# Row-wise inverse, Pool's large operations given to VectorE and ScalarE, the decay in the state update, and ScalarE in source order, in a one-layer RWKV-7 and Conformer step

## The chip, the cores and the metric

The kernel runs on one core of a Trainium2 chip. The metric is the device time of one execution in microseconds. The kernel before was timed three times: 1833.41, 1838.17 and 1839.06 us, median 1838.17. The engines are called by the profile's names: PE (TensorE, matrix products), PEld (its weight loads), DVE (VectorE), ACT (ScalarE), POOL (GpSimd) and SP (SyncE, which issues nearly all DMAs here).

## The reference, cut to what matters

520 columns are worked on together: 512 prompt tokens and 8 single decode tokens. After an RMSNorm, one product with `w_in` gives everything that the two branches need.

```python
proj = xn @ w_in                    # 2048 -> 3200 + 1024 + 2048 + 1024 + 4096
xs = p_shift + mu * (prev - p_shift)        # token shift, then r, k, v and two low ranks
decay = exp(-exp(w_log));  a = sigmoid(a0 + xa @ a_lora_b)
kk = k*k_k / max(norm(k*k_k), 1e-12);  kf = k * (1 + (a-1)*k_a)
# scan over tokens, 16 heads of 64 x 64 state:
S = S*w_t + (S a_t) b_t' + v_t k_t'         # a_t = -kk, b_t = kk*a
o_t = S r_t
o = groupnorm(o)*lnx_g + lnx_b + sum(r*kf*r_k)*v
y_a = (o * silu(gate_a)) @ w_proj_a
u = glu;  c = depthwise_conv31(u) + conv_b  # Conformer branch
y_b = (silu(layernorm(c)) * silu(gate_b)) @ w_proj_b
h = x + (sigmoid(ga)*y_a + sigmoid(gb)*y_b) @ w_out
h = h + sigmoid(h @ w_ple_gate) * (p @ w_ple);  y = rmsnorm(h)
```

All is float32. The scan also has an initial state for the 8 decode tokens; shifted rows, states and the last rows of the convolution's input are outputs as well.

## The kernel before, in words

**The large products.** Channels lie on the 128 partitions, the 520 columns along the free axis. Each tile of 128 output channels takes one `gemm` (L215), whose steps (`step`, L195) each multiply one 128 x 128 block of the weights with two halves of 260 columns. Both sides are split into a high and a low part (fp32r), so a step is three products of two halves, six matmuls. Weights come by DMA in tiles `w` (L141). For each group of four steps ACT writes the high part `wh` (L154), and DVE the low part `wl` (L169) by a subtraction. `wh` and `wl` have four buffers each; the high part is written three groups ahead of use (AHEAD, L31) and the low part is issued at the start of a later group (`lower`, L199).

**What lies beside them.** Everything else is written as Python generators that `tick` (L181) moves on by one piece after each step of a product. `yield 4` means "go on four steps later". `yield ROOM` means "go on when DVE has room": the program keeps a planned clock for PE and one for DVE, charges DVE `0.14 + 0.00107 n` us for an operation on n elements of a partition (L103), charges DVE `0.0007 n` us for an operation of POOL on more than 64 (L104), and holds a ROOM piece back while DVE's clock is over 1 us (LAG) ahead of PE's. This decides at build time in which order instructions are written. PE (L73) and, from L349 on, DVE keep that order on the chip (`manual_schedule`); the order of ACT, POOL and SP is chosen by the compiler's scheduler from its own cost model. On every engine instructions start in their queue's order, so one that waits holds back those behind it.

**One pass of `wkv` (L429), eight in all, two heads each.** It normalises `kk`, forms `ep` and `em` (running decays and their inverses, L480 to L484), `b`, `kf` (L488), `rk` and `bv` (the bonus, L503 to L506), and the scaled operands `ar` and `bk` (L511 to L518): per chunk of 64 tokens and head, rows of r, kk, kf and b times decays. Products of these, masked, give `nba`, `nbr` and the lower half of `ar` (L527 to L541). A 64 x 64 unit triangular matrix per chunk and head is inverted by its 32 x 32 diagonal blocks: the blocks go through DRAM (`nd`) into `ni`, one block on each partition; 31 steps of one multiplication `tm` and one sum `ti` (L566 to L571) build the inverse; it returns through DRAM (`td`) into `tts`, is transposed on DVE to `d11`, and matmuls form the off-diagonal block (`aux<-d,nba`, L587; `aux<-tts,yt`, L603). `ttb` holds the whole inverse. The loop over 8 chunks (L633 to L657) carries the state: four matmuls with `suv`, ACT copies `xs` (L640), one matmul per chunk with `ttb`, ACT copies into `suv` (L644), four matmuls with `bkt` and `nbr`, then DVE writes the next state twice, into `suv` and into `sf` (L653, L656). Between these three parts lie `ly` = 4 steps. The outputs are normalised per head, transposed, scaled by ACT to `og` (L689), and POOL adds `bv` and multiplies with the gate `sl` (L690, L691).

**What runs beside a pass.** `conv` (L713) makes 30 DVE operations on `c`, each a shifted multiply and add over 482 to 511 columns, all ROOM pieces. `scaled` (L370) empties a product's PSUM into `p`. `silu` (L393) and L918 have their products on POOL. While the last pass runs, `sample` (L751) does the decode tokens' state update with large operations of POOL and DVE. The helper lines L66 and L67 record every DVE, POOL and small-matmul instruction, so the profile shows them all under L67; they are told apart by the tiles' names.

Of the kernel before, what the change touches and what calls it, by code (L numbers as in the profile page):

```python
# [17 lines left out]
P = 128  # L18
# [52 lines left out]
def body(nc, tc, a):  # L71
    with ExitStack() as es:
# [34 lines left out]
        def tt(eng, out, x, y, op):  # L107
            eng.tensor_tensor(out, x, y, op=op)
# [240 lines left out]
        order.enter_context(tc.manual_schedule(engines={mybir.EngineType.DVE}))  # L349
# [60 lines left out]
        tts = kq.tile([P, NCH, 64], F32, name="tts")  # L410
        ttb = kq.tile([P, NCH, P], F32, name="ttb")
        nbrs = [kq.tile([P, NCH, P], F32, name=f"nbr{i}") for i in range(2)]
        for x in (tts, ttb, *nbrs):
            gps.memset(x, 0.0)
        d11 = kq.tile([P, NCH, 32], F32, name="d11")

        flag = {"samples": 0, "inv": -1, "done": -1, "loop": -1, "conv": 0, "yp": None, "merged": False}
# [11 lines left out]
        def wkv(p, box):  # L429
# [58 lines left out]
            gps.tensor_scalar(kf, av, col(O_KA, p), oka[:, p:p + 1], op0=ALU.mult, op1=ALU.add)  # L488
            tt(gps, kf, kf, k, ALU.mult)
            yield 5  # L490
# [3 lines left out]
            yield ROOM  # L494
            rk = gt("rk")
# [60 lines left out]
            gps.tensor_copy(epl, ep[:, :, 64])  # L556
            tt(gps, bh, bh, ep[:, :, 64:65].to_broadcast([P, NCH, P]), ALU.mult)
# [6 lines left out]
            gps.tensor_scalar(ti.rearrange("p i t -> p (i t)"), ttinit, 1.0, 0.0, op0=ALU.mult, op1=ALU.add)  # L564
            yield 3
            for t in range(1, 32):  # L566
                tm = kq.tile([P, 8, 32], F32, name="tm")
                tt(vec, tm[:, :, :t + 1], ti[:, :, :t + 1],
                   ni[:, 0:t + 1, t].unsqueeze(1).to_broadcast([P, 8, t + 1]), ALU.mult)
                vec.tensor_reduce(ti[:, :, t], tm[:, :, :t + 1], axis=AX.X, op=ALU.add)  # L570
                yield ROOM  # L571
            flag["inv"] = p
            for g in range(4):
                dma(out=td.rearrange("h c e i t -> (h c e) i t")[:, g * 8:(g + 1) * 8, :], in_=ti[g * 32:(g + 1) * 32])
            for h in range(2):
                for e in range(2):
                    dma(out=tts[h * 64 + e * 32:h * 64 + e * 32 + 32, :, e * 32:e * 32 + 32],
                        in_=td[h, :, e].rearrange("c i t -> i c t"))
            yield 16
            for h in range(2):  # L580
                vec.transpose(d11[h * 64:h * 64 + 32], tts[h * 64:h * 64 + 32, :, 0:32])
            yield 4
            o = aux().rearrange("p (c x) -> p c x", x=64)
            for c in range(NCH):
                for h in range(2):
                    x, y = quarter(2 * h), quarter(2 * h + 1)
                    pe.matmul(o[y, c, 0:32], lhsT=nba[x, c, 32:64], rhs=d11[x, c, :], start=True, stop=True)  # L587
# [12 lines left out]
            for c in range(NCH):  # L600
                for h in range(2):
                    x, y = quarter(2 * h), quarter(2 * h + 1)
                    pe.matmul(o[x, c, 0:32], lhsT=yt[y, c, :], rhs=tts[y, c, 32:64], start=True, stop=True)  # L603
            for h in range(2):
                s = half(h)
                gps.tensor_scalar(ttb[s, :, s], tts[s], 1.0, 0.0, op0=ALU.mult, op1=ALU.add)
# [24 lines left out]
            sf = kq.tile([P, 64], F32, name="sf", bufs=2)  # L631
            gps.memset(sf, 0.0)
            for c in range(NCH):  # L633
# [16 lines left out]
                if c + 1 < NCH:  # L650
                    for h in range(2):
                        s = half(h)
                        vec.scalar_tensor_tensor(suv[s, h, c + 1, :], sf[s], epl[s, c:c + 1], x[s, 3, :], op0=ALU.mult, op1=ALU.add)  # L653
                s0 = sf
                sf = kq.tile([P, 64], F32, name="sf", bufs=2)
                vec.scalar_tensor_tensor(sf, s0, epl[:, c:c + 1], x[:, 3, :], op0=ALU.mult, op1=ALU.add)  # L656
# [30 lines left out]
            og = gt("og")[:, :NPR]  # L687
# [4 lines left out]
            dma(out=oa_d[p, :, 0:NPR], in_=og)  # L692

# [19 lines left out]
        def conv(i, u):  # L713
# [417 lines left out]
```

## Time and profile before

| what | value |
|---|---|
| time of the profiled execution | 1836.85 us |
| its span, first to last instruction | 1835.1 us |
| median of the three runs | 1838.17 us |
| PE busy | 1785.5 us, 97% |
| DVE busy | 1279.5 us, 70% |
| ACT busy | 743.3 us, 41% |
| POOL busy | 353.3 us, 19% |

"Busy" is the union of an engine's instructions. Matmuls overlap one another, so a busy PE says that its queue did not run dry, and the number of matmuls in a stretch says how fast it went. The clock column (PEclk) is the share of full speed that the chip granted PE. In a row of waits stand the waiting instruction, what released it, the sum in us, how often, and the longest.

### The profile page before, as it was taken

The numbers are of one execution on the slowest core, as the hardware profiler recorded it, in microseconds if no ns is written. First come the engines' busy times: TensorE is split into PE (matmuls) and PEld (weight loads), VectorE is DVE, ScalarE is ACT, GpSimd is POOL, SyncE is SP. The second block draws the span as 40 slices with busy tenths as digits, with TensorE's granted clock in tenths as the row PEclk, the third lists the DMA queues.
The fourth block names the chain that finished last, engine by engine and source line by source line (L and its number), as shares of the span: only waits on it lengthen the run. The fifth ranks groups of instructions, "written<-read, shape, count | busy, mean of one in ns | idle before, by whom it ended". The sixth has DMA issues, their size and how long they took to land.

```text
span 1835.1 us, 37880 instructions
## 1 busy us (share of the span) xinstructions
PE 1785.5 (97%) x15576; PEld 1744.7 (95%) x15576; DVE 1279.5 (70%) x2300; ACT 743.3 (41%) x1355; POOL 353.3 (19%) x370
## 2 busy tenths in 40 slices
PE   9999999999999999999999999999999999999996
PEld 9999999999998999989999999999999999999995
DVE  6569999799798797896996998465444333334456
ACT  6735336244253363353362332454333222243354
POOL 1222203113113013032131155001022000011102
PEclk9999999999999999999999999999999999999998
DMA  6252322532432433324323344467555433362232
GB/s 232 84 133 79 107 93 79 114 92 74 119 103 68 112 96 98 96 80 107 94 84 104 122 131 149 130 225 238 192 179 185 123 116 98 93 195 93 93 104 94
DMA packets 121037, 220.49 MB, mean 120 GB/s; under 512 B 47888, under 2 KB 56208, under 8 KB 120864
## 3 DMA queue, kind: packets, MB, share of 16 engines
q1 hardware_dynamic: 119264, 216.47, 38.4%
q8 instruction: 122, 2.00, 0.4%
q10 hardware_dynamic: 1600, 1.60, 0.3%
q14 instruction: 51, 0.42, 0.1%
HBM read 188.69 MB, written 29.34 MB: 119 GB/s over the span
## 4 chain that ended last, share of the span: by engine, by line
PE 74%; DVE 19%; issue 3%; ACT 1%; POOL 1%; DMA 1%; SPq 0%; DVEq 0%; ACTq 0%; POOLq 0%
PE mm L211 68%; PE aux L67 5%; DVE wl L67 4%; DVE tm L67 4%; DVE c L67 3%; DVE ti L67 2%; PE aux L211 1%; DVE p L67 1%; DVE sq L67 1%; DVE on L67 1%; PE oc L67 1%; DMA w<-in_win 0%; DVE h L67 0%; DVE suv L67 0%; DVE m L67 0%
## 5 line engine op out<-in xcount | busy, mean ns | idle before, releaser
L154 ACT ACTIVATE wh<-w 128x512 fp32r<-128x512 f32 (+1 forms) x541 | 338.7, 628 | 627.5 <-PE mm L211 503.8
L211 PE MATMUL mm<-xh,wh 128*128 128x260 f32 x2784 | 589.1, 293 | 0.4 <-ACT xh L266 0.4
L211 PE MATMUL mm<-xh,wl 128*128 128x260 f32 x2784 | 565.9, 285 | 4.6 <-DVE wl L67 4.6
L211 PE MATMUL mm<-xl,wh 128*128 128x260 f32 x2784 | 566.0, 285 | 0.3 <-DVE xl L67 0.3
L67 DVE TENSOR_TENSOR wl<-w,wh 128x512 fp32r<-128x512 f32 (+1 forms) x541 | 397.5, 738 | 200.4 <-ACT wh L154 198.3
L211 PEld LDWEIGHTS mm<-xh,wh 128*128 128x128 f32 x2784 | 432.6, 191 | 12.1 <-ACT wh L154 0.6
L211 PEld LDWEIGHTS mm<-xh,wl 128*128 128x128 f32 x2784 | 433.7, 191 | 5.2 <-DVE wl L67 5.2
L211 PEld LDWEIGHTS mm<-xl,wh 128*128 128x128 f32 x2784 | 433.8, 191 | 0.6 <-DVE xl L67 0.5
L211 PE MATMUL mm<-hi,wl 128*128 128x260 f32 x1600 | 333.5, 284 | 2.6 <-DVE wl L67 2.6
L211 PE MATMUL mm<-hi,wh 128*128 128x260 f32 x1600 | 333.3, 283 | 0.0
L211 PE MATMUL mm<-lo,wh 128*128 128x260 f32 x1600 | 332.4, 282 | 0.0
L211 PEld LDWEIGHTS mm<-hi,wl 128*128 128x128 f32 x1600 | 250.7, 189 | 3.1 <-DVE wl L67 3.1
L211 PEld LDWEIGHTS mm<-hi,wh 128*128 128x128 f32 x1600 | 252.0, 189 | 0.1
L211 PEld LDWEIGHTS mm<-lo,wh 128*128 128x128 f32 x1600 | 251.8, 189 | 0.0
L67 DVE SCALAR_TENSOR_TENSOR c<-u,prm,c 128x482 f32<-128x482 f32 (+14 forms) x240 | 201.6, 840 | 4.4
L67 DVE TENSOR_TENSOR tm<-ti,ni 128x16 f32<-128x16 f32 (+30 forms) x248 | 104.1, 420 | 4.9
L67 POOL TENSOR_TENSOR sq<-hi,lo 128x520 f32<-128x520 f32 (+1 forms) x20 | 24.3, 1220 | 337.8 <-DVE one L67 184.0
L67 DVE TENSOR_TENSOR p<-mm,rs 128x520 f32<-128x520 f32 x78 | 53.7, 689 | 48.3 <-PE mm L211 48.2
L67 DVE TENSOR_REDUCE ti<-tm 128x8 f32<-128x16 f32 (+30 forms) x248 | 73.6, 297 | 8.5
L67 DVE TENSOR_TENSOR s<-mm,s 128x520 f32<-128x520 f32 x32 | 22.4, 700 | 65.9 <-PE mm L211 65.9
L67 POOL COPY nsh<-p 128x9 f32<-128x9 f32 x25 | 14.9, 597 | 238.0 <-DVE p L67 238.0
L67 DVE SCALAR_TENSOR_TENSOR suv<-sf,epl,aux 64x64 f32<-64x64 f32 x112 | 31.1, 278 | 38.4 <-PE aux L67 22.4
(233 smaller groups left out, 1652.5 us busy)
## 6 DMA issues: line engine op xcount, KB each, us to landing
w<-in_win SPq DMA_DIRECT2D x170, 512.0 KB, 3.7
w<-in_wout SPq DMA_DIRECT2D x32, 512.0 KB, 3.7
w<-in_wpg SPq DMA_DIRECT2D x24, 512.0 KB, 3.7
s<-sga_d SPq DMA_DIRECT2D x32, 260.0 KB, 2.8
w<-in_wpa SPq DMA_DIRECT2D x16, 512.0 KB, 3.8
w<-in_wpb SPq DMA_DIRECT2D x16, 512.0 KB, 3.8
wx<-in_wpg SPq DMA_DIRECT2D x32, 256.0 KB, 3.5
x<-in_xT SPq DMA_DIRECT2D x16, 260.5 KB, 5.7
```

The source lines that it names most:

```text
L67: return f(*args, **kw)
L154: behind.append(act(wh[:, k], w[:, k], AF.Copy))
L211: nc.tensor.matmul(o[h], lhsT=w[:, used[0] % 4, :], rhs=x[:, h * HF:(h + 1) * HF], start=(k == 0 and i == 0), stop=(k == nk - 1 and i == 2))
```

## The change

It does six things.

- **ACT in source order.** `manual_schedule` at L349 takes ACT as well as DVE: until the product with `w_proj_a` is done (L967) ACT's queue is in the order in which the program is written.
- **The inverse by rows.** The steps run from row 30 to row 0 and take `ni[:, t, t:]`, a contiguous row, where they took `ni[:, 0:t+1, t]`, a column with 32 elements between neighbours. Steps and lengths are the same (31, of 2 to 32 times 8 elements). The inverse comes back into `dtt`, and one DVE transpose of 128 partitions makes `dt`; before, two of 32 partitions made `d11`, and `tts` served as the other form.
- **POOL's large operations elsewhere.** To DVE: the product `kf*k`, half of `ar` and half of `bk` (four operations a pass), the two operations on `og` (now one fused multiply and add that reads PSUM, and one product), the decode columns' product in `conv` and the running sum `csum`. To ACT: `kf`'s scale and bias, `epl`, the initial `ti`, the four diagonal blocks of `ttb`, and the bias of `og`, now put on `bv`.
- **The decay in the state update.** `bk` is no longer multiplied by the chunk's decay. The update is `(x + S) * epl`: DVE forms `suv` from `x`, `epl` and an `sf` that ACT has already scaled; `sf` is no longer computed by DVE in each chunk.
- **No tile of its own for `og`.** It is written over `bv`. A pass waits, before `rk`, until the output of the pass two before it has been issued.
- **Some pauses** are moved or added (16 steps become 18 after the inverse, and ROOM stands before each product of `ar` and `bk`).

```diff
-        order.enter_context(tc.manual_schedule(engines={mybir.EngineType.DVE}))
+        order.enter_context(tc.manual_schedule(engines={mybir.EngineType.DVE, mybir.EngineType.Activation}))
...
-            gps.tensor_scalar(kf, av, col(O_KA, p), oka[:, p:p + 1], op0=ALU.mult, op1=ALU.add)
-            tt(gps, kf, kf, k, ALU.mult)
-            yield 5
+            act(kf, av, AF.Identity, scale=col(O_KA, p), bias=oka[:, p:p + 1])
+            yield 3
+            tt(vec, kf, kf, k, ALU.mult)
+            yield 1
...
             yield ROOM
+            while p > 1 and flag["out"] < p - 2:
+                yield 1
             rk = gt("rk")
...
+            act(bv[:, :NPR], bv[:, :NPR], AF.Identity, bias=col(O_LB, p))
...
                 tt(vec, ar[h][s, :, h, :], ch(kk)[s], ep[s, :, 0:64], ALU.mult)
-                tt(gps, ar[h][s, :, 1 - h, :], ch(r)[s], ep[s, :, 1:65], ALU.mult)
+                yield ROOM
+                tt(vec, ar[h][s, :, 1 - h, :], ch(r)[s], ep[s, :, 1:65], ALU.mult)
                 yield ROOM
                 tt(vec, bk[s, :, h, :], ch(b)[s], ch(em)[s], ALU.mult)
-                tt(gps, bk[s, :, 1 - h, :], ch(kf)[s], ch(em)[s], ALU.mult)
+                yield ROOM
+                tt(vec, bk[s, :, 1 - h, :], ch(kf)[s], ch(em)[s], ALU.mult)
...
-            gps.tensor_copy(epl, ep[:, :, 64])
-            tt(gps, bh, bh, ep[:, :, 64:65].to_broadcast([P, NCH, P]), ALU.mult)
+            act(epl, ep[:, :, 64], AF.Copy)
...
-            gps.tensor_scalar(ti.rearrange("p i t -> p (i t)"), ttinit, 1.0, 0.0, op0=ALU.mult, op1=ALU.add)
+            act(ti.rearrange("p i t -> p (i t)"), ttinit, AF.Copy)
...
-            for t in range(1, 32):
+            for t in range(30, -1, -1):
                 tm = kq.tile([P, 8, 32], F32, name="tm")
-                tt(vec, tm[:, :, :t + 1], ti[:, :, :t + 1],
-                   ni[:, 0:t + 1, t].unsqueeze(1).to_broadcast([P, 8, t + 1]), ALU.mult)
-                vec.tensor_reduce(ti[:, :, t], tm[:, :, :t + 1], axis=AX.X, op=ALU.add)
+                tt(vec, tm[:, :, t:], ti[:, :, t:], ni[:, t:t + 1, t:].to_broadcast([P, 8, 32 - t]), ALU.mult)
+                vec.tensor_reduce(ti[:, :, t], tm[:, :, t:], axis=AX.X, op=ALU.add)
                 yield ROOM
...
-                    dma(out=tts[h * 64 + e * 32:h * 64 + e * 32 + 32, :, e * 32:e * 32 + 32],
-                        in_=td[h, :, e].rearrange("c i t -> i c t"))
-            yield 16
-            for h in range(2):
-                vec.transpose(d11[h * 64:h * 64 + 32], tts[h * 64:h * 64 + 32, :, 0:32])
+                    dma(out=dtt[h * 64 + e * 32:h * 64 + e * 32 + 32], in_=td[h, :, e].rearrange("c t i -> t c i"))
+            yield 18
+            dt = kq.tile([P, NCH, 32], F32, name="dt")
+            vec.transpose(dt, dtt)
...
-                gps.tensor_scalar(ttb[s, :, s], tts[s], 1.0, 0.0, op0=ALU.mult, op1=ALU.add)
+            for q in map(quarter, range(4)):
+                act(ttb[q, :, q], dt[q], AF.Copy)
...
-                        vec.scalar_tensor_tensor(suv[s, h, c + 1, :], sf[s], epl[s, c:c + 1], x[s, 3, :], op0=ALU.mult, op1=ALU.add)
-                s0 = sf
-                sf = kq.tile([P, 64], F32, name="sf", bufs=2)
-                vec.scalar_tensor_tensor(sf, s0, epl[:, c:c + 1], x[:, 3, :], op0=ALU.mult, op1=ALU.add)
+                for h in range(2) if c + 1 < NCH else ():
+                    s = half(h)
+                    if c:
+                        vec.scalar_tensor_tensor(suv[s, h, c + 1, :], x[s, 3, :], epl[s, c:c + 1], sf[s], op0=ALU.mult, op1=ALU.add)
+                    else:
+                        vec.tensor_scalar(suv[s, h, 1, :], x[s, 3, :], epl[s, 0:1], None, op0=ALU.mult)
+                for h in range(2) if c + 1 < NCH else ():
+                    act(sf[half(h)], suv[half(h), h, c + 1, :], AF.Copy, scale=epl[half(h), c + 1:c + 2])
+                if c + 1 == NCH:
+                    vec.scalar_tensor_tensor(sf, x[:, 3, :], epl[:, c:c + 1], sf, op0=ALU.mult, op1=ALU.add)
...
-            act(og, ot, AF.Identity, scale=col(O_LG, p), bias=col(O_LB, p))
-            tt(gps, og, og, bv[:, :NPR], ALU.add)
-            tt(gps, og, og, sl[:, :NPR], ALU.mult)
+            yield 1
+            vec.scalar_tensor_tensor(og, ot, col(O_LG, p), bv[:, :NPR], op0=ALU.mult, op1=ALU.add)
+            tt(vec, og, og, sl[:, :NPR], ALU.mult)
...
-            tt(gps, tm, sc, cw.unsqueeze(1).to_broadcast([P, NS, 31]), ALU.mult)
+            tt(vec, tm, sc, cw.unsqueeze(1).to_broadcast([P, NS, 31]), ALU.mult)
...
-                tt(gps, csum, csum, c, ALU.add)
+                tt(vec, csum, csum, c, ALU.add)
```

More of the change, by code (lines that the diff above doesn't have):

```diff
@@ L408, in lowrank @@
             flag["low"] = True
-        tts = kq.tile([P, NCH, 64], F32, name="tts")
         ttb = kq.tile([P, NCH, P], F32, name="ttb")
         nbrs = [kq.tile([P, NCH, P], F32, name=f"nbr{i}") for i in range(2)]
-        for x in (tts, ttb, *nbrs):
+        for x in (ttb, *nbrs):
             gps.memset(x, 0.0)
-        d11 = kq.tile([P, NCH, 32], F32, name="d11")
-        flag = {"samples": 0, "inv": -1, "done": -1, "loop": -1, "conv": 0, "yp": None, "merged": False}
+        flag = {"samples": 0, "out": -1, "inv": -1, "done": -1, "loop": -1, "conv": 0, "yp": None, "merged": False}
         def firsts(box):
@@ L574, in wkv @@
                 dma(out=td.rearrange("h c e i t -> (h c e) i t")[:, g * 8:(g + 1) * 8, :], in_=ti[g * 32:(g + 1) * 32])
+            dtt = kq.tile([P, NCH, 32], F32, name="dtt")
             for h in range(2):
                 for e in range(2):
-                    dma(out=tts[h * 64 + e * 32:h * 64 + e * 32 + 32, :, e * 32:e * 32 + 32],
-                        in_=td[h, :, e].rearrange("c i t -> i c t"))
-            yield 16
-            for h in range(2):
-                vec.transpose(d11[h * 64:h * 64 + 32], tts[h * 64:h * 64 + 32, :, 0:32])
+                    dma(out=dtt[h * 64 + e * 32:h * 64 + e * 32 + 32], in_=td[h, :, e].rearrange("c t i -> t c i"))
+            yield 18
+            dt = kq.tile([P, NCH, 32], F32, name="dt")
+            vec.transpose(dt, dtt)
             yield 4
@@ L586, in wkv @@
                     x, y = quarter(2 * h), quarter(2 * h + 1)
-                    pe.matmul(o[y, c, 0:32], lhsT=nba[x, c, 32:64], rhs=d11[x, c, :], start=True, stop=True)
+                    pe.matmul(o[y, c, 0:32], lhsT=nba[x, c, 32:64], rhs=dtt[x, c, :], start=True, stop=True)
             yt = kq.tile([P, NCH, 32], F32, name="yt")
@@ L602, in wkv @@
                     x, y = quarter(2 * h), quarter(2 * h + 1)
-                    pe.matmul(o[x, c, 0:32], lhsT=yt[y, c, :], rhs=tts[y, c, 32:64], start=True, stop=True)
-            for h in range(2):
-                s = half(h)
-                gps.tensor_scalar(ttb[s, :, s], tts[s], 1.0, 0.0, op0=ALU.mult, op1=ALU.add)
+                    pe.matmul(o[x, c, 0:32], lhsT=yt[y, c, :], rhs=dt[y, c, :], start=True, stop=True)
+            for q in map(quarter, range(4)):
+                act(ttb[q, :, q], dt[q], AF.Copy)
             for h in range(2):
@@ L630, in wkv @@
             oc = aux("oc").rearrange("p (c x) -> p c x", x=64)
-            sf = kq.tile([P, 64], F32, name="sf", bufs=2)
-            gps.memset(sf, 0.0)
+            sf = kq.tile([P, 64], F32, name="sf")
             for c in range(NCH):
@@ L686, in wkv @@
                 pe.transpose(ot[:, c * P:(c + 1) * P], on[:, c, :], ident)
-            og = gt("og")[:, :NPR]
+            og = bv[:, :NPR]
             sl = box["sl"]
-            act(og, ot, AF.Identity, scale=col(O_LG, p), bias=col(O_LB, p))
-            tt(gps, og, og, bv[:, :NPR], ALU.add)
-            tt(gps, og, og, sl[:, :NPR], ALU.mult)
+            yield 1
+            vec.scalar_tensor_tensor(og, ot, col(O_LG, p), bv[:, :NPR], op0=ALU.mult, op1=ALU.add)
+            tt(vec, og, og, sl[:, :NPR], ALU.mult)
             dma(out=oa_d[p, :, 0:NPR], in_=og)
+            flag["out"] = p
         def gnorm(o, og, n):
@@ L725, in conv @@
             tm = et("tm")[:, :NS * 31].rearrange("p (b k) -> p b k", k=31)
-            tt(gps, tm, sc, cw.unsqueeze(1).to_broadcast([P, NS, 31]), ALU.mult)
             yield 5
+            yield ROOM
+            tt(vec, tm, sc, cw.unsqueeze(1).to_broadcast([P, NS, 31]), ALU.mult)
             vec.tensor_reduce(c[:, NPR:], tm, axis=AX.X, op=ALU.add)
@@ L739, in conv @@
             if i == 0:
-                gps.tensor_scalar(csum, c, 1.0, 0.0, op0=ALU.mult, op1=ALU.add)
+                act(csum, c, AF.Copy)
             else:
-                tt(gps, csum, csum, c, ALU.add)
+                tt(vec, csum, csum, c, ALU.add)
             flag["conv"] += 1
```

4 lines of the change are left out of this document (removed).

## The prediction, made before the changed kernel was run

> **What bounds the kernel now.** I read the page's first block, then the busy time by stretches, the clock, PE's waits in the slow stretch, and last the instructions around two waits.
>
> ```profile
> span 1835.1 us, 37880 instructions
> PE 1785.5 (97%) x15576; PEld 1744.7 (95%) x15576; DVE 1279.5 (70%) x2300; ACT 743.3 (41%) x1355; POOL 353.3 (19%) x370
> ```
> ```profile
> 150.00:1100.00 950.00, 920.23 (x8373) 885.81 (x8372) 820.77 (x1563) 390.79 (x760) 225.02 (x253) 0.98 0.34 98
> 1200.00:1790.00 590.00, 590.00 (x4918) 589.89 (x4917) 263.42 (x395) 213.34 (x353) 58.84 (x41) 1.00 0.46 147
> 1790.00:1836.00 46.00, 27.16 (x202) 25.69 (x201) 30.83 (x53) 18.62 (x34) 9.96 (x11) 0.81 0.28 94
> ```
> ```profile
> core 0: 1835.1 us, clock 0.986
> ```
>
> In the stretch rows the columns are the length, then busy time and count of PE, PEld, DVE, ACT and POOL, then the clock. From 1200 to 1790 us PE never idles: 4918 matmuls in 590 us, 0.120 us each. Nothing of the change can win there. From 150 to 1100, where the eight passes run, PE idles 950 - 920.23 = 29.8 us, and DVE is busy 820.77 / 950 = 86%. The clock is below 1 there too: over the span 1835.1 x 0.014 = 25.7 us of full clock are missing, of which the tail has 46 x 0.19 = 8.7, so 17 us are missing in the passes. Together 29.8 + 17 = 46.8 us can be won, if every wait of PE and every dip of the clock in that stretch goes.
>
> PE's own waits from 150 to 1100 name who is late (a row of 0.4 us is left out):
>
> ```profile
> PE aux L67 <- DVE d L67: 8.9, 11, 2.2
> PE aux L67 <- ACT suv L644: 5.5, 2, 3.0
> PE mm L211 <- DVE wl L67: 4.6, 3, 2.0
> PE aux L67 <- ACT xs L640: 4.1, 3, 1.9
> PE aux L67 <- DVE suv L67: 3.4, 2, 1.8
> PE aux L67 <- ACT yt L591: 2.5, 3, 2.2
> ```
>
> These are few and long waits, 1 to 3 us. The longest, at 566 us, shows why. First PE and the clock around it, then DVE and POOL just before (start, length, what):
>
> ```profile
> 560.00:566.00 6.00, 3.44 (x29) 3.23 (x28) 5.96 (x5) 0.61 (x2) 4.65 (x4) 0.98 0.18 51
> 566.00:570.00 4.00, 3.58 (x21) 3.46 (x22) 3.90 (x9) 3.29 (x7) 0.44 (x1) 0.50 0.14 55
> ```
> ```profile
> 566.42 0.48 PE L67 MATMUL aux<-suv,bkt 128*64 128x64 f32 x4 [2.98 <-ACT suv L644]
> ```
> ```profile
> 561.90 1.78 DVE L67 TENSOR_TENSOR wl<-w,wh 128x512 fp32r<-128x512 f32 x1
> 563.60 1.75 DVE L67 SCALAR_TENSOR_TENSOR rk<-r,prm,a 128x520 f32<-128x520 f32 x1
> 565.28 1.52 DVE L67 SCALAR_TENSOR_TENSOR c<-u,prm,c 128x508 f32<-128x508 f32 x2
> 566.72 0.69 DVE L67 TENSOR_TENSOR p<-mm,rs 128x520 f32<-128x520 f32 x1
> ```
> ```profile
> 560.13 1.30 POOL L67 TENSOR_TENSOR a<-a,k 128x520 f32<-128x520 f32 x1
> 561.51 3.29 POOL L67 TENSOR_TENSOR bk<-a,cs 64x512 f32<-64x512 f32 x2
> ```
> ```profile
> 567.12 5.50 PE mm L211 x24
> 576.71 2.93 PE mm L211 x24
> ```
>
> While POOL makes `a*k` and the two halves of `bk`, DVE takes 1.78 and 1.75 us for operations of a size that takes 0.69 to 0.76 right after: these two alone lose 2 us of the 2.98 for which PE then waits. ACT stood between (it waited for `rk`), so the wait carries ACT's name. Then the clock is 0.50 for 4 us, and the chain of waits has 24 matmuls at 5.50 us instead of 2.93. So a late DVE costs twice: the wait, and the clock after it.
>
> [...]
>
> **The change part by part.** Durations are means of groups:
>
> ```profile
> L67 DVE TENSOR_TENSOR tm<-ti,ni 128x16 f32<-128x16 f32 (+30 forms) x248 | 104.1, 420 | 4.9
> L67 DVE TENSOR_REDUCE ti<-tm 128x8 f32<-128x16 f32 (+30 forms) x248 | 73.6, 297 | 8.5
> L67 DVE SCALAR_TENSOR_TENSOR sf<-sf,epl,aux 128x64 f32<-128x64 f32 x64 | 17.9, 280 | 6.9 <-PE aux L67 5.1
> L67 DVE STREAM_TRANSPOSE d<-tts 32x256 f32<-32x256 f32 x16 | 6.9, 431 | 0.3
> L67 DVE TENSOR_TENSOR ar<-aux,cst 64x512 f32<-64x512 f32 x32 | 22.0, 688 | 0.4
> L67 DVE TENSOR_TENSOR lo<-x,hi 128x520 fp32r<-128x520 f32 x16 | 11.2, 701 | 1.7
> L67 DVE SCALAR_TENSOR_TENSOR rk<-r,prm,a 128x520 f32<-128x520 f32 x8 | 12.9, 1610 | 3.3 <-POOL a L67 3.2
> L67 DVE SCALAR_TENSOR_TENSOR r<-p,omu,q 128x520 f32<-128x520 f32 x8 | 6.0, 755 | 0.1
> L67 DVE SCALAR_TENSOR_TENSOR c<-u,prm,c 128x482 f32<-128x482 f32 (+14 forms) x240 | 201.6, 840 | 4.4
> L67 DVE SCALAR_TENSOR_TENSOR c<-u,prm,c 128x489 f32<-128x489 f32 x8 | 5.8, 723 | 0.1
> L67 POOL TENSOR_TENSOR sl<-p,sg 128x520 f32<-128x520 f32 x8 | 12.9, 1608 | 19.0 <-ACT sg L396 18.8
> ```
>
> *Added to DVE, per pass.* Four products for `ar` and `bk` and two operations for `og` at 0.69 (the `ar` row), `kf*k` and `csum` at 0.70 (the `lo` row), the decode product in `conv` at 0.4 (248 elements; on the line between 0.297 for 136, the mean size of the `ti` row, and 0.688 for 512 lies 0.41). 6 x 0.69 + 2 x 0.70 + 0.4 = 5.9 us.
>
> *Taken from DVE, per pass.* Seven of eight `sf`: 7 x 0.28 = 2.0. One of two transposes: 0.4. In the inverse both operations of a step have the same number of elements, but the multiplication, which reads a column of `ni`, takes 0.420 and the sum 0.297. The trace has no multiplication of a row: it lies between 0.297 and 0.420, and I take 0.30, since the plan's 0.14 + 0.00107 n, which gives the `ar` row's 0.688 for 512, gives 0.29 for 136. 31 x 0.12 = 3.7 (bounds 0 and 3.8).
>
> *Collisions with POOL.* 0.840 in place of 0.723 is 0.117 x 240 = 28 us on `c`, and (1.610 - 0.755) x 8 = 6.8 on `rk`: 35 us on these two alone, 4.4 per pass, with `wl` and others not counted. Three large products per pass stay on POOL (the two of `silu`, and L918; about 1.6 us each by the `sl` row), and the decode tokens' operations. I count two thirds, 2.9 per pass (bounds 0 and 4.4). The net on DVE is 5.9 - 2.0 - 0.4 - 3.7 - 2.9 = -3.1 us per pass, 25 us in all out of 820.77. DVE stays near 86% of a shorter stretch; its sum is not what wins.
>
> *What wins is that DVE is late at fewer points.* PE consumes a piece four steps after it was issued: 24 matmuls, 2.93 us. DVE may be that late and no more. The plan decides how late it gets. It charges 0.36 us for a POOL operation on 512 columns, which in the rows above cost DVE about 1.05; the six between `b` and `bk` in one pass are therefore up to 6 x 0.7 = 4 us too cheap. After the change five DVE operations stand there, charged 0.69 and lasting 0.69 or 0.70, four of them behind ROOM. The inverse is charged 62 x (0.14 + 0.00107 x 136) = 17.7 us and lasts 31 x (0.420 + 0.297) = 22.2: DVE is 4.5 us behind plan at its end, and `og` (two operations of POOL) and `ttb` follow just there, ahead of `d`, which PE waits for most. With the row form it is 31 x 0.60 = 18.6, so 0.9 behind, and neither of the two is on POOL. Both excesses exceeded 2.93; both fall below it. So nearly all rows of PE's waits lose their cause. I leave a quarter for what stays on POOL, for `conv` (30 operations charged 0.67, lasting 0.72) and for the decode tokens: 0.75 x 46.8 = 35.1 us won.
>
> *ACT.* These rows price what it gets:
>
> ```profile
> L644 ACT ACTIVATE suv<-aux 64x64 f32<-64x64 f32 x128 | 27.8, 217 | 58.8 <-PE aux L67 54.6 <-DVE ti L67 1.9 <-DVE tm L67 1.2
> L608 ACT ACTIVATE ttb<-aux 32x256 f32<-32x256 f32 x16 | 6.0, 374 | 7.8 <-PE aux L67 7.5
> L730 ACT ACTIVATE c<-u,prm 128x512 f32<-128x512 f32 x8 | 6.5, 816 | 6.6 <-DMA c_d<-c 3.0 <-DVE u L67 2.7 <-DMA w<-in_win 0.7
> L480 ACT ACT_TABLE_LOAD x8 | 10.3, 1283 | 0.1
> L480 ACT ACTIVATE ep<-cs 128x512 f32<-128x512 f32 x8 | 5.1, 633 | 0.1
> ```
> ```profile
> ACT wh L154 <- PE mm L211: 524.4, 317, 4.6
> ```
>
> `kf` 0.82 (L730), four `ttb` blocks 4 x 0.37, fourteen `sf` copies at 0.22 to 0.32 (L644; a scale read from memory may add something) 3 to 4.5, `ti` 0.37, `epl` 0.2; the bias on `bv` replaces `og`'s. About 6.5 us per pass, 52 us, on an engine busy 390.79 of 950: it is hidden, because ACT waits 524 us for PE to free a `wh`. If that cover were gone, 52 us would be the price.
>
> *ACT's order* is the part whose price no row shows. A gain: `wh` no longer stands ahead of a copy that PE needs sooner. A loss: an ACT instruction whose DVE input is late holds back all behind it. New waits of that kind are the `sf` copies and the bias on `bv`. Queued behind them are the next `wh`, which has three groups of 2.93 us of cover, and `xs` and `suv` of the loop, which have one. Bounds: 10 us won, 46 lost (below). I take 0, nearest the rows in which ACT waits for PE.
>
> *With one answer.* DMAs stay four for four of the same size on SP's queue, in the same place; the two extra steps before the transpose lie beside the previous pass's loop; the wait for the output two passes back comes after a whole loop of eight chunks, so it is met when reached, and if not only `rk` moves later, with PE still on its products. All these: 0. The small matmuls are the same in number and size.
>
> **The sum.** 1836.85 - 35.1 = 1801.8 for the profiled execution; the median of the runs stands 1.3 above it, so 1803.
>
> **The rivals.**
>
> *ACT's queue becomes the late one (slower).* Place: after the reciprocal in each pass ACT now has in one piece a table load, two exponentials, a small one and `kf`: 1.28 + 0.63 + 0.63 + 0.2 + 0.82 = 3.6 us, and similar pieces at `silu` and at the square roots. If ACT arrives there 1 us late because it waited for DVE, an `xs` or `suv` behind it comes 3.6 + 1 - 2.93 = 1.7 us late for PE. Three such pieces in eight passes are 24 x 1.7 = 41 us, and the clock dips stay at 17: 1836.85 - 46.8 + 41 + 17 = 1848. It decides from ACT being 2.93 us late at a copy of the loop. For it: PE's waits for `xs`, `suv` and `yt` already make 12.1 us. Against: they come from a late DVE, which the change removes.
>
> *The lateness stays (no change).* If the row form is no faster and collisions on `sl` and the like weigh as much as those removed, DVE has 5.9 - 2.4 - 0 to 2 = 1.5 to 3.5 us more per pass and is as late as today: 1837. For it: DVE at 86%. Against: the plan knows of operations on DVE and pauses others.
>
> *Only half goes.* Without the row form's gain the 8.9 us before `d` and a third of the dips stay, 8.9 + 5.7: 1801.8 + 14.6 = 1816. [...]
>
> **How the numbers follow.** The forecast has 0.58 (its own range 1790, all won, to 1810). Only half: 0.20, of which the clock's rule 0.05. No change 0.09, slower 0.13. A measurement of this kernel tells about 0.3% (5.5 us) from no change. Faster is 0.58 + 0.20 = 0.78. The range starts at 1788, where all that idles is won, and reaches over the half cases to 1830, leaving out the last two rivals.
>
> **What would show it.** DVE's `rk` falls from 1.61 to about 0.76, `c` from 0.84 to below 0.76; `tm` falls from 0.420 to about 0.30; PE's wait for `d` nearly goes; the clock in the stretch of the passes is 0.99 or 1.00; POOL's busy time falls by more than a third and ACT's rises by about 50 us. The prediction is wrong if PE still idles 25 us or more among the passes, and the slower rival is right if those waits are for `xs` and `suv` with DVE idle.

## The result, and the profile after

| | before | after |
|---|---|---|
| median of four runs each | 1836.59 us (1833.41 to 1839.06) | 1793.62 us (1792.67 to 1796.86) |
| profiled execution | 1836.85 us | 1793.73 us |

The ratio after to before is 0.977, 95% interval 0.9749 to 0.9791: 43 us faster. The prediction had said 1803 us, 1788 to 1830.

First the top of the page of the changed kernel, then the tail and the stretch of the eight passes by their busy times (length, then busy time and count of PE, PEld, DVE, ACT and POOL, then the clock):

```profile
span 1791.9 us, 37772 instructions
...
PE 1766.2 (99%) x15576; PEld 1728.4 (96%) x15576; DVE 1240.0 (69%) x2307; ACT 778.6 (43%) x1509; POOL 197.3 (11%) x241
```
```profile
1745.00:1792.00 47.00, 28.54 (x225) 27.18 (x223) 32.34 (x55) 20.13 (x37) 9.97 (x11) 0.88 0.28 96
150.00:1100.00 950.00, 944.27 (x8743) 911.19 (x8742) 818.09 (x1622) 442.68 (x940) 108.53 (x153) 1.00 0.35 105
```
```profile
core 0: 1791.9 us, clock 0.996
```

Read the second of the two stretch rows by PE's count. In the same 950 us PE made 8743 matmuls in place of 8373; 370 more at 0.120 us each are 44.4 us, about the whole gain (43.1 between the two profiled executions). PE's idle time there went from 29.8 us to 950 - 944.27 = 5.7, and the clock from 0.98 to 1.00. Over the span 1791.9 x 0.004 = 7.2 us of clock are missing, and 47 x 0.12 = 5.6 of these lie in the tail. So 17 us became 1.6. Read in slices of half a microsecond, the clock shows the same more exactly: among the passes of the kernel before it stood at 0.50 in seven dips for 34.1 us together, which loses 17.1 us, and in the changed kernel in one dip of 3.41 us, which loses 1.7. Idle time and clock together give 24.1 + 15.4 = 39.5 us; the other 3.6 of the 43.1 these rows don't place. DVE is as busy as before in this stretch (818 us against 821), but does more of the work in it: its sum over the span fell by 39.5 us.

PE's own waits from 150 to 1100 us, to be held against the six rows of before:

```profile
PE aux L67 <- ACT suv L645: 2.8, 4, 2.3
PE mm L211 <- DVE wl L67: 1.7, 3, 1.0
PE aux L67 <- DVE lo L67: 0.7, 1, 0.7
PE aux L67 <- ACT xs L641: 0.3, 1, 0.3
```

(A row of 0.2 us is left out.) The wait for `d`, 8.9 us before, has no row any more. The groups of instructions (busy time, mean ns of one, then idle time before them):

```profile
L67 DVE TENSOR_TENSOR wl<-w,wh 128x512 fp32r<-128x512 f32 (+1 forms) x541 | 390.0, 723 | 208.3 <-ACT wh L154 206.3 <-PE mm L211 1.2
L67 DVE SCALAR_TENSOR_TENSOR c<-u,prm,c 128x482 f32<-128x482 f32 (+14 forms) x240 | 181.5, 756 | 4.4
L67 DVE TENSOR_TENSOR tm<-ti,ni 128x16 f32<-128x16 f32 (+30 forms) x248 | 79.1, 319 | 8.5 <-ACT ti L567 3.1
L659 ACT ACTIVATE sf<-suv,epl 64x64 f32<-64x64 f32 x112 | 38.6, 345 | 85.9 <-DVE suv L67 84.5
L67 DVE SCALAR_TENSOR_TENSOR rk<-r,prm,a 128x520 f32<-128x520 f32 x8 | 6.0, 755 | 0.0
L608 ACT ACTIVATE ttb<-dt 32x256 f32<-32x256 f32 x32 | 13.2, 411 | 0.3
```

`rk` fell from 1610 to 755 ns, `c` from 840 to 756, `tm` from 420 to 319. These are signs that the prediction had named.

### The profile page after: what moved, and what is told of

Read it like the earlier page. It is cut to its first block, busy times and chain, and to the rows that moved or that the text cites. A ratio compares the mean times of both kernels' runs of the same rounds, so it can differ in the third digit from the quotient of the medians.

```text
span 1791.9 us, 37772 instructions
## 1 busy us (share of the span) xinstructions
PE 1766.2 (99%) x15576; PEld 1728.4 (96%) x15576; DVE 1240.0 (69%) x2307; ACT 778.6 (43%) x1509; POOL 197.3 (11%) x241
## 4 chain that ended last, share of the span: by engine, by line
PE 90%; DVE 6%; ACT 2%; issue 1%; DMA 0%; DVEq 0%; SPq 0%; ACTq 0%
PE mm L211 83%; PE aux L67 5%; DVE c L67 2%; PE aux L211 1%; DVE wl L67 1%; PE oc L67 1%; DVE h L67 0%; DVE p L67 0%; DVE tm L67 0%; ACT wh L154 0%; DVE ti L67 0%; DMA w<-in_wfst 0%; ACT L478 0%; DVE rf L67 0%; DMA w<-in_win 0%
## 5 line engine op out<-in xcount | busy, mean ns | idle before, releaser
L67 DVE TENSOR_TENSOR wl<-w,wh 128x512 fp32r<-128x512 f32 (+1 forms) x541 | 390.0, 723 | 208.3 <-ACT wh L154 206.3
L211 PEld LDWEIGHTS mm<-xh,wl 128*128 128x128 f32 x2784 | 428.5, 189 | 2.4 <-DVE wl L67 2.3
L211 PEld LDWEIGHTS mm<-xl,wh 128*128 128x128 f32 x2784 | 429.1, 189 | 0.3 <-DVE xl L67 0.2
L67 DVE SCALAR_TENSOR_TENSOR c<-u,prm,c 128x482 f32<-128x482 f32 (+14 forms) x240 | 181.5, 756 | 4.4
L67 DVE TENSOR_TENSOR tm<-ti,ni 128x16 f32<-128x16 f32 (+30 forms) x248 | 79.1, 319 | 8.5 <-ACT ti L567 3.1
L659 ACT ACTIVATE sf<-suv,epl 64x64 f32<-64x64 f32 x112 | 38.6, 345 | 85.9 <-DVE suv L67 84.5
L645 ACT ACTIVATE suv<-aux 64x64 f32<-64x64 f32 x128 | 27.8, 217 | 80.6 <-PE aux L67 79.1
L67 DVE SCALAR_TENSOR_TENSOR suv<-aux,epl,sf 64x64 f32<-64x64 f32 x96 | 27.1, 282 | 49.8 <-PE aux L67 47.1
```

The lines of the kernel that those rows point to most:

```text
L67: return f(*args, **kw)
L211: nc.tensor.matmul(o[h], lhsT=w[:, used[0] % 4, :], rhs=x[:, h * HF:(h + 1) * HF], start=(k == 0 and i == 0), stop=(k == nk - 1 and i == 2))
L645: act(suv[half(h), h, c, :], x[half(h), 2, :], AF.Copy)
L659: act(sf[half(h)], suv[half(h), h, c + 1, :], AF.Copy, scale=epl[half(h), c + 1:c + 2])
```

## The experiments

The theory under test: the time went because DVE was late against the plan by more than PE's cover, and the change brought what DVE really takes close to what the plan charges. The main rival: DVE simply had too much to do, and the change took work from it. Further theories concern single parts: ACT's order, the freed matmul, the clock. The runs in one table, each with its ratio to runs of the kernel before on the same chip:

| kernel | median, us | ratio (95%) |
|---|---|---|
| before, rows alone | 1808.85 | 0.9846 (0.9831 to 0.9862) |
| before, both charges of the plan corrected | 1799.87 | 0.9804 (0.9783 to 0.9825) |
| before, the column's charge alone | 1809.15 | 0.9854 (0.984 to 0.9868) |
| changed, inverse by columns | 1812.08 | 0.9864 (0.9848 to 0.9879) |
| changed, matmul behind DVE again | 1796.73 | 0.9785 (0.9771 to 0.9798) |
| changed, operations back on POOL | 1803.71 | 0.9823 (0.9797 to 0.9848) |
| before, ACT in source order | 1837.55 | 0.9999 (0.9989 to 1.001) |
| changed, ACT's order free | 1791.77 | 0.9754 (0.9737 to 0.9772) |
| changed, with 14 pauses | 1858.21 | one run |
| ACT free, decode tokens later in the source | 1791.55 | 0.9758 (0.9737 to 0.9779) |
| ACT free, higher charge for POOL | 1791.57 | 0.9758 (0.9744 to 0.9772) |
| ACT free, decode later, POOL in source order | 1786.92 | 0.9733 (0.9719 to 0.9747) |

**The inverse by rows alone, in the kernel before.** All else stays, but for the transpose, and POOL copies the diagonal blocks in four quarters.

```diff
-            for t in range(1, 32):
+            for t in range(30, -1, -1):
...
-                tt(vec, tm[:, :, :t + 1], ti[:, :, :t + 1],
-                   ni[:, 0:t + 1, t].unsqueeze(1).to_broadcast([P, 8, t + 1]), ALU.mult)
+                tt(vec, tm[:, :, t:], ti[:, :, t:], ni[:, t:t + 1, t:].to_broadcast([P, 8, 32 - t]), ALU.mult)
...
-                vec.transpose(d11[h * 64:h * 64 + 32], tts[h * 64:h * 64 + 32, :, 0:32])
+            vec.transpose(dt, dtt)
```

> The kernel before with only the inverse by rows (and the one transpose that goes with it; the diagonal blocks are still copied by POOL). Theory: the waits before the first small matmul (8.9 us) go, those around rk and bk stay, 1815 to 1830 us. Rival (POOL alone makes DVE late): 1832 us or more. Rival (the rows alone win): 1805 us or less.

Measured 1808.85 us, 1.5% below before: more than was expected. The multiplication by a row takes 311 ns here (420 by a column), while `rk` is still slow:

```profile
L67 DVE TENSOR_TENSOR tm<-ti,ni 128x16 f32<-128x16 f32 (+30 forms) x248 | 77.0, 311 | 5.0
L67 DVE SCALAR_TENSOR_TENSOR rk<-r,prm,a 128x520 f32<-128x520 f32 x8 | 11.4, 1422 | 2.0 <-POOL a L67 2.0
```
```profile
PE aux L67 <- ACT suv L640: 9.8, 5, 3.0
```

The 27 us that `tm` gives back (104.1 - 77.0) come through about one for one, though POOL's collisions are nearly as they were (`c` takes 857 ns, 840 before). The wait for `d` is gone, but here, too, PE's first matmul behind the inverse reads what the DMA brought, so it could not wait for DVE's transpose; one for `suv` is the longest now. This run can't say whether the shorter work or the better agreement with the plan wins.

**The kernel before, with the plan told the truth.** The instructions stay the same; only what the plan charges changes, and with it the order. The wait for the output two passes back, which the changed kernel has too, is added.

```diff
-        gps = Paced(nc.gpsimd, lambda name, n: work(0.0007 * n if n > 64 else 0.05))
+        gps = Paced(nc.gpsimd, lambda name, n: work(0.0013 * n if n > 64 else 0.05))
...
+            while p > 1 and flag["out"] < p - 2:
+                yield 1
...
                    ni[:, 0:t + 1, t].unsqueeze(1).to_broadcast([P, 8, t + 1]), ALU.mult)
+                work(0.0008 * 8 * (t + 1))
```

> The kernel before, same operations on the same engines, with only the plan's charges changed: POOL's operations 0.0013 us an element in place of 0.0007, and 0.0008 us more for each element that the inverse's multiplication reads by columns (and the wait for the output two passes back, without which the order cannot be laid out). Theory (PE waits because DVE is later than the plan knows): with true charges DVE's ROOM pieces step back and most waits go though DVE does the same work, 1795 to 1818 us. Rival (DVE simply has too much to do in those places, whatever the plan says): 1828 us or more.

Measured 1799.87 us: 2.0% won, of the 2.3% that the whole change wins. Of the three groups on which the prediction rested, `c` and `tm` are as slow as before, and `rk` takes 1428 ns, far from the 755 of the changed kernel:

```profile
L67 DVE SCALAR_TENSOR_TENSOR c<-u,prm,c 128x482 f32<-128x482 f32 (+14 forms) x240 | 200.3, 835 | 4.5 <-DMA ni<-nd 1.4
L67 DVE TENSOR_TENSOR tm<-ti,ni 128x16 f32<-128x16 f32 (+30 forms) x248 | 105.4, 425 | 4.2
L67 DVE SCALAR_TENSOR_TENSOR rk<-r,prm,a 128x520 f32<-128x520 f32 x8 | 11.4, 1428 | 7.3 <-POOL a L67 7.2
```
```profile
150.00:1100.00 950.00, 941.26 (x8697) 908.50 (x8696) 845.78 (x1605) 404.90 (x785) 239.90 (x266) 1.00 0.35 103
```
```profile
PE aux L67 <- ACT xs L643: 3.5, 1, 3.5
PE aux L67 <- ACT suv L647: 2.0, 2, 1.7
PE aux L67 <- DVE d L67: 1.2, 2, 1.1
```

PE idles 8.7 us where it idled 29.8, with DVE busier in the stretch than before (845.78 us; 820.77), because more of the work fits into it; over the span DVE's sum is 1274.1 us, and 1279.5 before. The rival, too much work on DVE, falls: with the same work most of the gain is there. PE waits 1.2 us for `d` where it waited 8.9. DVE is not done with the inverse any sooner for that: from its first `tm` to its last the inverse takes 39.0 us here, 36.7 before (means of the eight passes). What moved is the order. Charged more, the plan holds DVE's ROOM pieces back, the inverse's own steps among them, and so sets the matmul that reads `d` behind more products: from the start of the inverse to that matmul PE makes 419 matmuls of the large products on average, and 379 before. The 40 between them last 4.8 us at 0.120 us each. The wait for the output two passes back was not tried without the charges. Nor was any other way to slow the plan, say a smaller LAG, so these runs do not tell a true charge from one that is merely higher.

**The column's charge alone.** POOL's charge goes back to 0.0007.

> The kernel before, with one of the two corrected charges alone: 0.0008 us more for each element of the inverse's multiplications by a column (527 x 8 elements, 3.4 us in a pass), POOL's charge as it was. Theory: lateness is a sum, so that each charge wins its share; with both the kernel took 1799.9 us against 1836: 1808 to 1825 us with this one. Rival: the inverse alone is what was late (inverse by rows alone won 28 us too): 1799 to 1806 us. Third: POOL's charge did it, the column's adds nothing: 1830 us or more.

Measured 1809.15 us, 27.8 below the 1836.99 of before beside it. That is about what rows alone won (29.8 against 1838.62). The charge adds 527 x 8 x 0.0008 = 3.4 us to a pass; rows take 3.4 us from it ((104.1 - 77.0) / 8). So it makes little difference whether the inverse becomes as short as the plan thinks, or the plan as long as the inverse is. In this run PE still reads DVE's transpose `d` and waits 0.5 us for it in all. The inverse takes 37.0 us, as before, but the matmul comes 399 large matmuls behind its start. On top of this charge POOL's wins another 9 us; POOL's charge alone was not run.

**The changed kernel with the inverse by columns.** Nothing else is taken back, but with columns the first small matmul's operand is again a transpose of DVE's.

```diff
-            for t in range(30, -1, -1):
+            for t in range(1, 32):
...
-            dt = kq.tile([P, NCH, 32], F32, name="dt")
-            vec.transpose(dt, dtt)
+            dtt = kq.tile([P, NCH, 32], F32, name="dtt")
+            vec.transpose(dtt, dt)
```

> The changed kernel with the inverse by columns again; the DVE transpose then makes the operand of the first small matmul, as in the kernel before, so PE waits for DVE there. Theory: DVE ends the inverse about 4 us behind its plan, PE's wait for that operand comes back in part, 1798 to 1812 us. Rival (the rows are worth nothing, all is POOL's): 1791 to 1797 us.

Measured 1812.08 us, 18 above the changed kernel. The multiplication is back at 429 ns, and a wait before the inverse's matmul is back:

```profile
L67 DVE TENSOR_TENSOR tm<-ti,ni 128x16 f32<-128x16 f32 (+30 forms) x248 | 106.5, 429 | 9.0 <-ACT ti L567 3.5
```
```profile
PE aux L67 <- DVE dtt L67: 3.9, 4, 2.4
```

**The freed matmul by itself.** In the changed kernel `aux<-dtt,nba` reads what the DMA brought, and no longer waits for DVE. Here it reads a second transpose.

```diff
             vec.transpose(dt, dtt)
+            dtv = kq.tile([P, NCH, 32], F32, name="dtv")
+            vec.transpose(dtv, dt)
...
-                    pe.matmul(o[y, c, 0:32], lhsT=nba[x, c, 32:64], rhs=dtt[x, c, :], start=True, stop=True)
+                    pe.matmul(o[y, c, 0:32], lhsT=nba[x, c, 32:64], rhs=dtv[x, c, :], start=True, stop=True)
```

> The changed kernel, but the first small matmul of the inverse reads a transpose that DVE makes (one more transpose of 128x256 behind the one that is there), where the changed kernel's reads what the DMA brought. It asks how much of the rows' gain is that TensorE no longer stands behind DVE at that matmul. Theory: the gain is the inverse's shorter time on DVE, and the matmul's freedom is worth little: two transposes instead of one cost DVE some 0.3 us in each of 8 passes, 1794 to 1800 us. Rival: the freedom is most of the 18 us that the inverse by columns costs the changed kernel: 1803 to 1812 us, and the wait for the new operand heads the list of TensorE's waits with 4 to 9 us.

Measured 1796.73 us, 3 above the changed kernel (the intervals overlap). PE waits 0.8 us for `dtv` in all:

```profile
PE aux L67 <- DVE dtv L67: 0.8, 1, 0.8
```

By the medians the freedom is worth about 3 us, so some 15 of the 18 belong to the multiplication. The overlap leaves both open by a few us.

**POOL's operations back on POOL, in the changed kernel.** The inverse by rows, the state update and ACT's order stay.

```diff
-            act(kf, av, AF.Identity, scale=col(O_KA, p), bias=oka[:, p:p + 1])
...
-            tt(vec, kf, kf, k, ALU.mult)
+            gps.tensor_scalar(kf, av, col(O_KA, p), oka[:, p:p + 1], op0=ALU.mult, op1=ALU.add)
+            tt(gps, kf, kf, k, ALU.mult)
...
-                tt(vec, bk[s, :, 1 - h, :], ch(kf)[s], ch(em)[s], ALU.mult)
+                tt(gps, bk[s, :, 1 - h, :], ch(kf)[s], ch(em)[s], ALU.mult)
...
-            tt(vec, og, og, sl[:, :NPR], ALU.mult)
+            tt(gps, og, og, sl[:, :NPR], ALU.mult)
```

The same is done with the halves of `ar`, `epl`, `ti`, the blocks of `ttb`, the decode product and `csum`.

> The changed kernel with kf, its product with k, the halves of ar and bk, the gate product of og, epl, ti, the diagonal blocks of ttb, the decode product and csum on POOL again; rows, state update and ACT's order stay. Theory (collisions with POOL and the column reading each make DVE late, and the two add): PE's waits around rk and bk come back as in the kernel before with only the rows, 1804 to 1814 us, rk at 1.4 us or more. Rival (the rows were all, the rest is worth nothing): 1791 to 1797 us.

Measured 1803.71 us: 10 us for these moves, at the lower edge of what was expected. `c` is back at 839 ns, and `rk` takes 1280 ns, less than expected:

```profile
L67 DVE SCALAR_TENSOR_TENSOR rk<-r,prm,a 128x520 f32<-128x520 f32 x8 | 10.2, 1280 | 3.4 <-POOL a L67 3.4
```

**ACT's order.** It was put into the kernel before, alone, and taken out of the changed one, alone.

```diff
-        order.enter_context(tc.manual_schedule(engines={mybir.EngineType.DVE}))
+        order.enter_context(tc.manual_schedule(engines={mybir.EngineType.DVE, mybir.EngineType.Activation}))
```

> The kernel before with only ACT put in source order. Theory: DVE is as late as before, so 1828 to 1840 us. Rival (ACT's order wins): 1815 us or less.

> The changed kernel with ACT's order left to the scheduler again (only DVE and PE in source order). Theory (PE waited because DVE was late, from operations beside POOL and from the column reading): ACT's order is worth little, 1790 to 1802 us, PE idle among the passes below 12 us. Rival (the order of ACT is what won: the copies xs, suv and yt no longer stand behind a wh): most of the gain is lost, 1815 us or more, with PE's waits for xs, suv and yt back at about 12 us.

Measured 1837.55 us (ratio 0.9999, interval 0.9989 to 1.001) for the first and 1791.77 for the second, against 1793.62; the intervals of these last two overlap. In the first the wait for `d` stands as before:

```profile
PE aux L67 <- DVE d L67: 9.1, 14, 2.2
```

ACT's order is worth nothing that can be measured here, alone or with the rest.

**Pauses of PE, and the clock behind them.** To see what a wait does to the clock, 14 waits of PE for DVE, 2.09 to 4.15 us long, are put between the columns of the product with `w_out`, where PE never idles otherwise: one small matmul, a reciprocal of n columns on DVE, a copy, and one more matmul, whose results nothing uses.

```diff
+            if j % 15:
+                n = (64, 130, 200, 260, 330, 390, 460)[(j - 1) % 7]
...
+                vec.reciprocal(z[:, :n], o[:, :n])
+                vec.tensor_copy(zb, z[:, n - 64:n])
+                o = aux("pq")
+                nc.tensor.matmul(o[:, :64], lhsT=onb[:, :P], rhs=zb, start=True, stop=True)
             tt(vec, v2(x), gemm(16, ms), v2(x), ALU.add)
```

> The changed kernel with 14 pauses of PE put into the product with w_out, where PE otherwise never waits: before each of 14 output tiles PE makes one small matmul, DVE takes reciprocals of n of its elements (n = 64, 130, 200, 260, 330, 390, 460, twice), and PE's next matmul reads the result. Outputs are unchanged. [...]

Five of the waits (the matmul behind the wait, its idle time in brackets), and the six microseconds behind each of them, with the clock in the third column from the right:

```profile
1393.66 0.19 PE L1008 MATMUL pq<-zb,onb 128*128 128x64 bf16 x1 [2.51 <-DVE zb L67]
...
1409.27 0.19 PE L1008 MATMUL pq<-zb,onb 128*128 128x64 bf16 x1 [2.32 <-DVE zb L67]
...
1440.28 0.20 PE L1008 MATMUL pq<-zb,onb 128*128 128x64 bf16 x1 [2.90 <-DVE zb L67]
1455.65 0.20 PE L1008 MATMUL pq<-zb,onb 128*128 128x64 bf16 x1 [3.34 <-DVE zb L67]
...
1490.58 0.23 PE L1008 MATMUL pq<-zb,onb 128*128 128x64 bf16 x1 [4.15 <-DVE zb L67]
```
```profile
1393.66:1399.66 6.00, 6.00 (x38) 6.00 (x38) 0.69 (x1) 0.63 (x1) 0.00 (x0) 0.72 0.30 87
1409.27:1415.27 6.00, 6.00 (x51) 6.00 (x51) 1.24 (x2) 0.73 (x2) 0.00 (x0) 1.00 0.26 87
...
1440.28:1446.28 6.00, 6.00 (x51) 6.00 (x52) 1.23 (x2) 0.74 (x2) 0.00 (x0) 1.00 0.26 90
1455.65:1461.65 6.00, 6.00 (x38) 6.00 (x39) 1.23 (x2) 0.63 (x1) 0.00 (x0) 0.72 0.30 90
...
1490.58:1496.58 6.00, 6.00 (x28) 6.00 (x29) 0.63 (x2) 0.63 (x1) 0.00 (x0) 0.50 0.29 87
```

0.72 over six microseconds is half the clock for 3.4 of them; 51 matmuls become 38, so one dip costs about 1.6 us. After 2.51 us there is a dip, after 2.90 us there is none. Length alone does not decide. The trace shows a grid: the single dips last 3.41 us, the first of the two waits of 4.15 us comes with 6.83 us of half clock, and all dips begin a whole number of 3.413 us apart (read in slices of 0.25 us: 1394.35, 1425.07, 1455.79, 1472.85, 1489.91 us, which is 95.56 us for 28 steps, and four later ones). The seven dips among the passes of the kernel before have the same lengths: four last 3.41 us and three 6.83. On the grid of these starts the wait of 2.51 us lies within one step, from 1390.94 to 1394.35, while the wait of 2.90 us is cut by a boundary at 1438.72 into 1.34 and 1.56 us. All 14 waits fall into line: the five without a dip leave PE idle for at most 1.64 us of any one step, and the nine with one for at least 2.01 us. So in this run the idle time within one step of the grid tells the waits with a dip from those without, and the divide lies between 1.64 and 2.01 us of 3.41. What lies behind the grid was not shown.

**What is left in the changed kernel.** Most of what PE still waits among the passes (4.0 of 5.7 us) lies between 1016 and 1036 us, where the last pass's `conv` meets the decode tokens' products on POOL. Three ways were tried, each with ACT's order free. First POOL's operations are charged 0.0013, as was done above to the kernel before:

> The changed kernel with ACT's order left to the scheduler, and POOL's operations charged in the plan with 0.0013 us an element instead of 0.0007. Theory: lateness against the plan was the loss, and in the changed kernel nearly nothing of it is left in the passes; what is left at 1015 to 1036 us is charged too little still, so the higher charge can win 1 to 3 us: 1788 to 1791 us. Rival: the charge only spreads the same work and costs steps elsewhere: 1792 us or more.

Measured 1791.57 us, against 1791.77 without it: the same, and nothing of the 1 to 3 us expected. Next the old charge, with the decode tokens begun later in the source:

```diff
-            yield 12
+            while flag["conv"] < 8:
+                yield 1
             yield from samples()
```

> The changed kernel with ACT's order left to the scheduler and with the decode tokens' update started only when the last convolution is done, so that POOL's operations on it meet an emptier DVE. Theory: the waits between 1000 and 1036 us (4.7 us and a dip of the clock of 1.7 us) go, 1784 to 1790 us. Rival (the later start makes the normalisation after it late, and PE waits there): 1795 us or more.

Measured 1791.55 us: the same again, and a miss. POOL still ran these products from 1002 to 1016 us, since the scheduler chooses POOL's order: the place in the source meant nothing to it. Last the later place with POOL's order taken from the source, too:

```diff
-        order.enter_context(tc.manual_schedule(engines={mybir.EngineType.DVE, mybir.EngineType.Activation}))
+        order.enter_context(tc.manual_schedule(engines={mybir.EngineType.DVE, mybir.EngineType.Pool}))
```

> The changed kernel with ACT's order left to the scheduler, the decode tokens begun in the source only behind the eighth pass's convolution, and POOL's order, too, taken from the source. In the run before this one, with the later place alone, POOL still ran the decode tokens' products at 1002 to 1015 us, because its order was the scheduler's. Theory: the waits of TensorE that are left at 1015 to 1036 us come of these products' overlap with DVE's work, and go when POOL runs them later: 1784 to 1789 us. Rival: the decode tokens' work collides with DVE wherever it stands, or POOL in the source's order holds up other work: 1791 us or more.

Measured 1786.92 us (1786.51 to 1788.65), on the same chip as the 1791.57 (1790.26 to 1792.94) of the higher charge, and the fastest of all kernels here. The interval of its ratio (0.9719 to 0.9747) and that of the later place alone (0.9737 to 0.9779, on another chip) just overlap. POOL now runs five of the nine products at 1001 to 1009 us and the other four from 1040 on. DVE in the changed kernel, and in this one:

```profile
1010.13 4.87 DVE L67 SCALAR_TENSOR_TENSOR c<-u,prm,c 128x493 f32<-128x493 f32 x3
1014.92 1.78 DVE L67 TENSOR_TENSOR wl<-w,wh 128x512 fp32r<-128x512 f32 x1
```
```profile
1009.26 2.26 DVE L67 SCALAR_TENSOR_TENSOR c<-u,prm,c 128x493 f32<-128x493 f32 x3
1011.43 0.69 DVE L67 TENSOR_TENSOR wl<-w,wh 128x512 fp32r<-128x512 f32 x1
```

The twenty microseconds behind, first in the changed kernel, then with ACT's order free and the later place alone, and last in this one:

```profile
1020.00:1040.00 20.00, 16.47 (x128) 15.55 (x127) 18.46 (x30) 7.47 (x16) 0.00 (x0) 0.91 0.38 120
```
```profile
1020.00:1040.00 20.00, 17.29 (x150) 16.39 (x151) 17.35 (x28) 7.70 (x17) 0.00 (x0) 1.00 0.43 134
```
```profile
1020.00:1040.00 20.00, 19.52 (x174) 18.84 (x173) 15.27 (x25) 6.64 (x16) 0.18 (x1) 1.00 0.41 132
```

Of the 46 matmuls more than in the changed kernel, 22 are there already without POOL's order; the other 24, 2.9 us at 0.120 each, are what POOL's order gives in this stretch.

## Why the prediction was right, and where its sizes were off

**What can be won, 46.8 us, and three quarters of it, 35.1.** The bound held. The share was too small: 1836.85 - 1793.73 = 43.1 us were won. The quarter left over was 11.7 us; by the rows 5.7 us of idle time and 1.7 of clock still stand among the passes, and by the time only 3.7 are missing. That term is the one mis-sized, and 8.0 of the 9 us by which the forecast came out too high are its; the rest is the 1.3 us by which the median was set above the profiled execution. The term stood for the POOL operations that remain, for `conv` and for the decode tokens. Most of the idle time that is left stands behind the decode tokens' products, and the run that moves four of them on POOL is 4.6 us faster than the one beside it.

**Late by more than the cover of 2.93 us.** That DVE's lateness against the plan, and not its work, is what PE waits for is the step that carries the result, and the charges show it without touching DVE's work. The length of the cover was not varied in any run, so the 2.93 us themselves stay an argument. The two excesses, 4 us from POOL and 4.5 from the inverse, were taken for alike. They are not: the inverse alone wins 28 to 30 us in the kernel before, POOL's part another 9 or 10. The corrected charges fall short of the change by 0.3% or so, and the two intervals overlap; the work taken from DVE may be that, but no run separates it.

**DVE's sum.** It fell by 39.5 us, not by 25. What had been put down to collisions with POOL was more than had been taken. `c` and `rk`, for which 4.4 us a pass was the upper bound, became shorter by 20.1 and 6.9 us, 3.4 a pass, where two thirds of the bound, 2.9, had been counted. But the others, which had been named and not counted, gave 21.6 us more: `wl` 7.5 us (397.5 in the trace of before), `b` 3.9, and `bk`, `ar`, `on`, `k`, `kk` and `lo` 10.2 together, so that all of them make 6.1 a pass. `tm` gave 25.0 us, 3.1 a pass, and 3.7 had been said (319 ns and not 300). That the sum is not what wins was right.

**The wait for `d`.** The prediction laid its going to the shorter inverse and overlooked that PE no longer reads DVE's transpose there at all. That cost the forecast little: by the run with the second transpose it is worth about 3 us.

**ACT.** It rose by 35.3 us and not by 52. `sf` takes 345 ns, above the 220 to 320 that had been bounded from `suv`; the scale read from memory, which had been named as open, may be the reason; no run separates it. The blocks of `ttb` take 411 ns, not 370. Against these I count 47 table loads in the trace where before had 62, at 1283 ns each 19 us less. They go with ACT's order: with it free, the changed kernel has 66 loads and ACT is busy 809.7 us, 66 more than before. So what ACT was given was priced too low, and the order hid that. The work itself was hidden as said: ACT's waits for PE at `wh` fell from 524 to 371 us. ACT's order is worth 0 to the time, as taken; the bounds of 10 won and 46 lost were both far off.

**The rivals.** ACT's late queue did not come: the copies `suv` and `xs` cost 3.1 us of waits together. That only half goes is what the kernel by columns shows, 1812.08 us where 1816 had been worked out, but the nearness is partly luck: the columns cost 18 us and not 14.6, on a base 9 us lower, and PE waits 3.9 us for the operand, not 8.9; longer waits for `suv` (5.0 us) and others stand in its place, with 6.8 us lost to the clock. The chance of 0.05 for the clock's rule stood for a clock that stays low when the waits go. No run shows such a rule: the waits went and the clock came back with them, 0.98 to 1.00.

## What to carry to other kernels

Where a program decides its order from planned costs, compare each cost with the trace before making any operation faster: two wrong constants held most of what this change won, and correcting them took no work from any engine. DVE was 86% busy here and not the bound: with the charges corrected it was 89% busy in the same stretch (845.78 of 950 us), and PE waited less. Look for the places where such an engine is later than the engine that it feeds can cover. And an order that one engine keeps from the source is worth little if the engine that disturbs it keeps its own.

## What the runs showed of the hardware

A dip of the clock behind a pause of PE costs a further 1.6 us or so, and pauses of nearly the same length fall on either side: 2.51 us with one, 2.90 us without. In the one run with pauses the dips lie on a fixed grid of 3.413 us, and a pause had one where it left PE idle for 2.01 us or more of one step of this grid, and none at 1.64 us or less.

Next to large operations of POOL on the decode tokens, `c` and `wl` of the changed kernel keep POOL's pace rather than their own: three `c` take 4.87 us, or 1.62 each, and a `wl` 1.78, where 2.26 us, or 0.75 each, and 0.69 suffice with POOL idle (the run with POOL's order from the source). These are POOL's operations beside the three:

```profile
1009.73 1.63 POOL L67 TENSOR_TENSOR s<-s,sv 128x512 f32<-128x512 f32 x1
1011.32 1.47 POOL L67 TENSOR_TENSOR t<-sv 128x512 f32<-128x512 f32 x1
1012.75 1.72 POOL L67 TENSOR_TENSOR t<-s,sv 128x512 f32<-128x512 f32 x1
```

That one shuts the other out for its whole length does not show here. Three `c` alone take 2.26 us, and the shortest of POOL's products of these three kinds in the changed kernel 1.29, 1.04 and 1.28 us, 5.87 us for all six; side by side the three `c` took 4.87 us. This is one stretch of one run, so it stays open.

A broadcast multiplication that reads one operand with 32 elements between neighbours takes 420 to 429 ns where a contiguous row takes 311 to 319, at the same sizes (31 forms, 248 instructions).
